# A seven-product matmul form on two of four column tiles in every pair of weight columns

## The chip, the cores and the metric

The kernel runs on one core of one Trainium2 chip. The metric is device time in microseconds for one execution, the median of several runs. The kernel before takes 2792.92 us (three runs, 2792.88 to 2793.01).

## What is computed

Two layers of a decoder trunk on 256 tokens, width 2048, all in fp32. The large products, which are nearly all of the work, are these (x is 256 x 2048):

```python
for i in range(DEPTH):                       # 2 layers
    h = rmsnorm(x, norm_mix_g[i])
    proj = h @ w_in[i]                       # conv input, q, k, v, forget logits, two gates
    y_conv = conformer_conv(...)             # ends in  u @ w_conv_out
    y_attn = forgetting_attention(...) @ w_attn_out[i]
    merged = sigmoid(g_conv) * y_conv + sigmoid(g_attn) * y_attn
    x = x + merged @ w_out[i]                # 2048 x 2048
    hf = rmsnorm(x, norm_ffn_g[i])
    gate, up = split(hf @ w_gate_up[i])      # 2 x 2048 x 5632
    x = x + (silu(gate) * up) @ w_down[i]    # 5632 x 2048
    hp = rmsnorm(x, norm_ple_g[i])
    x = x + sigmoid(hp @ w_ple_gate[i]) * (p[i] @ w_ple_proj[i])
return rmsnorm(x, final_g)
```

## The kernel before

**Tiles.** The 256 tokens are two row blocks of 128. A weight matrix is cut into column tiles of 512 columns, and each column tile into groups of 512 rows (four slices of 128 rows). A group is one load of two pieces of 128 x 1024 (two slices side by side, 512 KB), fetched on SP's queue into one of 8 `raw` tiles (line 135).

**fp32 by halves.** Every weight piece is split into a high half (ScalarE copy to `wh`, line 141, 5 buffers) and a low half (VectorE subtraction to `wl`, line 142, 5 buffers). The activations are split once in the same way. A product of a piece is then three matmuls per slice and row block: high x high (line 184), high x low (185), low x high (186), each 128 x 128 against 512 columns. I call the making of `wh` and `wl` for one piece a split.

**Plain steps.** A plain step takes one piece: two slices, two row blocks, three matmuls, so 12 matmuls for one split. A group is two plain steps per column tile.

**The seven-product form.** `fast_chunks` (line 238) does a pair of column tiles `w1`, `w2` (1024 columns) at once, into two PSUM accumulators `c1` and `c2` (one for each column tile, two banks each). Over the reduction there are groups; the text calls a group *fast* where it uses seven products of two slices for the two column tiles and two row blocks, in place of eight (the 2 x 2 form with 7 multiplications). For a fast group (lines 274 to 292) the pieces are a11, a12 (from w1), sm and a22 (from w2); GpSimd's queue adds a11 onto sm in memory by an accumulating DMA (line 276); VectorE makes two sums and one difference of pieces (lines 287, 289, 291); and seven products follow, each of one split and 6 matmuls. So a fast group is 7 splits, 3 further VectorE operations and 42 matmuls, against 4 splits and 48 matmuls for the same group in plain steps. Four products have PSUM banks of their own, `p1`, `q5`, `q6`, `q7`, which is all four banks of the pool `pms`; they are read out once per pair (lines 293 to 297) into two SBUF tiles `u1`, `u2`, and joined with `c1` and `c2` (lines 300 and 304).

**Order in a pair.** The plain steps wait in the list `left`, all of w1's first, then w2's. Inside each fast group one or two of them are put between the products (lines 280 to 283). After the last fast group, `u1` and `u2` are made, the rest of w1's steps run, `c1` is added, `first(u1)` is called, then w2's steps.

**Turns.** A result must be transposed on TensorE to be an operand of the next product: a *turn* (8 transposes of line 334 through two `pms` banks, then for a plain group a ScalarE high half and a VectorE low half, lines 321 and 322; for a group that is to be fast, `Fast.take` and `Fast.make`, lines 349 to 377, with the sums of operands). Turns wait in a queue and are run after a plain step, though not while a pair is in its fast groups (`state["quiet"]`), or at once where a step needs the operand (`await_x`, line 210).

**Who uses it.** In each layer, 24 calls of `fast_chunks`:

- mixer gates (line 850): 4 pairs, 2 fast and 2 plain groups;
- `w_out` (lines 891 to 898): 2 pairs. The operands of groups 0 and 3 of `merged` are made for the fast form; the first pair uses 1 fast group, the second 2;
- gate/up (line 925): column tiles c = 1 to 10 of the hidden width (c = 0 is done in plain steps), in three parts of 3, 4 and 4. The first tile of parts two and three (c = 3, c = 7) uses 1 fast group, the others 2;
- `w_down` (line 936): after each part, 2 pairs over that part's 3 or 4 groups. Part one uses 1 fast group in both, parts two and three use 1 in the first pair and 2 in the second;
- `w_ple_gate` (line 1000): 2 pairs, 1 fast group in the first and 2 in the second. Before each pair come two short products of 12 matmuls (`w_ple_proj`).

The Tile framework orders each engine's instructions by priority (program order) among those that its own model finds ready, so the order on an engine is near program order but not the same.

I write GU3 for the gate/up pair of c = 3, D1.0 and D1.2 for the two down pairs of part 1 (parts are 0, 1, 2), O0 and O2 for the `w_out` pairs and P0 and P2 for the PLE gate pairs.

Of the kernel before, what the change touches and what calls it, by code (L numbers as in the profile page):

```python
# [45 lines left out]
def trunk(ctx, tc, xT, xR, pT, wI, wF, wC, wA, wOut, wGU, wD, wPG, wPP, vec, bF, gF, out):  # L46
# [191 lines left out]
    def fast_chunks(fast, w1, w2, xs, ks, first, by_block=None):  # L238
# [10 lines left out]
        for w, sums in ((w1, (c11, c12)), (w2, (c21, c22))):  # L249
            for g, k0 in enumerate(ks):  # L250
                for half in range(2):
                    left.append((w[len(fast) + g][:, half * 1024 : (half + 1) * 1024], sums, k0 + 2 * half))
# [20 lines left out]
        u1, u2 = pair(), pair()  # L273
        for g, f in enumerate(fast):
# [17 lines left out]
            product(c12, f(B22), a12)  # L292
        act.activation(u1[:, 0, :], p1.t, AF.Copy)
# [5 lines left out]
        go(len(left) - 2 * len(ks))  # L299
# [245 lines left out]
    for i in range(L):  # L545
# [319 lines left out]
        fast_merged = {0: Fast(), 3: Fast()}  # L865
# [25 lines left out]
        for n in range(0, N4, 2):  # L891
            by = (0, 1, 2, 3) if n == 0 else (0, 3, 1, 2)
            onto_x(norm, n + 1)(
                fast_chunks(
                    [fast_merged[g] for g in by[: 1 + n // 2]], *([wOut[i, m][g] for g in by] for m in (n, n + 1)),
                    merged, [4 * g for g in by[1 + n // 2 :]], onto_x(norm, n),
                )
            )
# [4 lines left out]
        for part, nch in enumerate(FFN_PARTS):  # L903
            hid = {}
            fast_hid = [Fast() for _ in range(nch - 2)]
            for c in range(c0, c0 + nch):
# [10 lines left out]
                if c == 0:  # L917
                    gate(chunk(by_four(w1), norm.xs))
                    up = chunk(by_four(w2), norm.xs)
                else:  # L920
                    nf = 1 if c == c0 else 2
                    up = fast_chunks(norm.fast[:nf], w1, w2, norm.xs, range(4 * nf, KD, 4), gate)
# [8 lines left out]
            for n in range(0, N4, 2):  # L931
                await_x(hid, (4 * c0,))
                on = after if part == len(FFN_PARTS) - 1 else None
                nf = 1 if n == 0 else len(fast_hid)
                onto_x(on, n + 1)(
                    fast_chunks(
                        fast_hid[:nf], wD[i, n][c0 : c0 + nch], wD[i, n + 1][c0 : c0 + nch], hid,
                        range(4 * (c0 + nf), 4 * (c0 + nch), 4), onto_x(on, n),
                    )
                )  # L940
# [53 lines left out]
        for n in range(0, N4, 2):  # L994
            for m in range(2):
# [5 lines left out]
                norm.fast[: 1 + n // 2], wPG[i, n], wPG[i, n + 1], norm.xs, range(4 + 2 * n, KD, 4), embedded(n),  # L1001
# [65 lines left out]
```

## Time and profile before

| | |
|---|---|
| median of three runs | 2792.92 us |
| the profiled execution's own time | 2793.7 us |
| its span (first to last instruction) | 2791.8 us |
| TensorE busy | 2773.9 us, 12568 matmuls |
| VectorE busy | 2507.1 us, 3003 instructions |
| ScalarE busy | 1660.0 us, 2002 instructions |
| splits on VectorE (line 142) | 1254, 1219 ns each |
| accumulating DMAs on GpSimd's queue | 80 |
| DMA in all | 585.24 MB, 210 GB/s |

The busy time of an engine is the union of its instructions' spans. A matmul's recorded duration (about 390 ns) overlaps the next one's, so the pace of TensorE is read from starts, not from durations. A row of the stretches view gives, for one stretch of the execution, its length and then each engine's busy time in it with the count of instructions that touch it.

### The profile page before, as it was taken

Reading aid. Unit: us, or ns where it says so; the run is one execution under the profiler, and the core shown is the slowest. Engines: PE = TensorE matmul, PEld = TensorE weight load, DVE = VectorE, ACT = ScalarE, POOL = GpSimd, SP = SyncE. Lnnn points to the kernel's source line nnn. Section 1 sums busy time; section 2 is a strip of 40 time slices with the busy share of each in tenths; the row PEclk is TensorE's granted clock in tenths of the full one; section 3 lists DMA queues with packets and bytes.
Section 4 is the critical chain, followed back from the end, with each engine's and each line's share of the span. In section 5 each row is a group of like instructions: output and inputs, shape, how many; then the busy total and the mean of one; then the engine's idle time right before and its main releaser. Section 6 shows DMA issues by size and latency. Waiting matters only on the chain.

```text
span 2791.8 us, 34941 instructions
## 1 busy us (share of the span) xinstructions
PE 2773.9 (99%) x12568; PEld 2293.5 (82%) x12568; DVE 2507.1 (90%) x3003; ACT 1660.0 (59%) x2002; POOL 79.4 (3%) x121
## 2 busy tenths in 40 slices
PE   9999999999999999999999999999999999999998
PEld 7888888888888888888888888888888888888886
DVE  7999889888989988999979988988799899889998
ACT  7445766565556655656754466655665565556565
POOL 0000000000000000000000000000000000000000
PEclk9999999999999999999999999999999999999999
DMA  7555557666676766776655555575666677677674
GB/s 299 188 182 185 199 186 227 198 217 201 217 226 220 227 218 220 224 221 203 215 186 190 185 181 199 189 233 184 228 205 215 216 232 231 203 229 218 217 239 131
DMA packets 161597, 585.24 MB, mean 210 GB/s; under 512 B 18192, under 2 KB 18448, under 8 KB 161168
## 3 DMA queue, kind: packets, MB, share of 16 engines
q1 hardware_dynamic: 149040, 539.50, 56.5%
q0 software_dynamic: 11520, 41.95, 8.3%
q8 instruction: 98, 1.61, 0.2%
q10 hardware_dynamic: 864, 1.57, 0.2%
q14 instruction: 75, 0.61, 0.1%
HBM read 580.85 MB, written 2.10 MB: 209 GB/s over the span
## 4 chain that ended last, share of the span: by engine, by line
PE 93%; DVE 3%; issue 3%; ACT 1%; POOL 0%; POOLq 0%; ACTq 0%; DVEq 0%
PE mm L186 25%; PE mm L185 25%; PE mm L184 25%; PE ms L184 5%; PE ms L185 5%; PE ms L186 5%; PE ms L334 2%; DVE wl L142 1%; DVE raw L271 0%; PE ms L726 0%; ACT wh L141 0%; PE ms L755 0%; DVE pair L374 0%; PE ms L745 0%; DVE pair L271 0%
## 5 line engine op out<-in xcount | busy, mean ns | idle before, releaser
L141 ACT ACTIVATE wh<-raw 128x1024 fp32r<-128x1024 f32 x1254 | 1300.5, 1058 | 1022.7 <-PE mm L186 576.7
L142 DVE TENSOR_TENSOR wl<-raw,wh 128x1024 fp32r<-128x1024 f32 x1254 | 1501.0, 1219 | 212.4 <-ACT wh L141 204.9
L184 PE MATMUL mm<-wh,pair 128*128 128x512 f32 x3224 | 1261.9, 392 | 1.1 <-ACT pair L324 0.7
L185 PE MATMUL mm<-wl,pair 128*128 128x512 f32 x3224 | 1256.6, 390 | 0.9 <-DVE wl L142 0.8
L186 PE MATMUL mm<-wh,pair 128*128 128x512 f32 x3224 | 1256.8, 390 | 0.5 <-DVE pair L325 0.5
L186 PEld LDWEIGHTS mm<-wh,pair 128*128 128x128 f32 x3224 | 605.2, 188 | 128.4 <-DVE pair L325 1.4
L185 PEld LDWEIGHTS mm<-wl,pair 128*128 128x128 f32 x3224 | 605.6, 188 | 126.3 <-DVE wl L142 3.2
L184 PEld LDWEIGHTS mm<-wh,pair 128*128 128x128 f32 x3224 | 605.4, 188 | 126.0 <-ACT pair L324 1.7
L184 PE MATMUL ms<-wh,pair 128*128 128x512 f32 x680 | 265.7, 391 | 0.1
L186 PE MATMUL ms<-wh,pair 128*128 128x512 f32 x680 | 264.7, 389 | 0.0
L185 PE MATMUL ms<-wl,pair 128*128 128x512 f32 x680 | 264.6, 389 | 0.0
L569 DVE SCALAR_TENSOR_TENSOR pair<-pair,vecs,pair 128x256 f32<-128x256 f32 x480 | 201.1, 474 | 0.0
L271 DVE TENSOR_TENSOR raw<-raw,raw 128x1024 f32<-128x1024 f32 x160 | 195.4, 1222 | 2.6
L184 PEld LDWEIGHTS ms<-wh,pair 128*128 128x128 f32 x680 | 127.7, 188 | 28.0 <-ACT pair L998 0.9
L186 PEld LDWEIGHTS ms<-wh,pair 128*128 128x128 f32 x680 | 127.6, 188 | 26.7
L185 PEld LDWEIGHTS ms<-wl,pair 128*128 128x128 f32 x680 | 127.7, 188 | 26.0
L272 DVE TENSOR_TENSOR raw<-raw,raw 128x1024 f32<-128x1024 f32 x80 | 98.0, 1225 | 2.6
L271 DVE TENSOR_TENSOR pair<-pair,ms 128x512 f32<-128x512 f32 x144 | 93.9, 680 | 0.0
L272 DVE TENSOR_TENSOR pair<-mm,pair 128x1024 f32<-128x1024 f32 (+1 forms) x48 | 58.1, 1210 | 11.5 <-PE mm L186 11.4
L271 DVE TENSOR_TENSOR pair<-pair,mm 128x1024 f32<-128x1024 f32 x48 | 58.3, 1215 | 5.5 <-PE mm L186 5.5
L374 DVE TENSOR_TENSOR pair<-pair,pair 128x1024 fp32r<-128x1024 f32 x52 | 62.8, 1217 | 0.0
L373 ACT ACTIVATE pair<-pair 128x1024 fp32r<-128x1024 f32 x52 | 54.3, 1055 | 2.7 <-DVE pair L364 1.6
(168 smaller groups left out, 1065.0 us busy)
## 6 DMA issues: line engine op xcount, KB each, us to landing
raw<-in_wGU_dram SPq DMA_DIRECT2D x352, 512.0 KB, 4.8
raw<-in_wI_dram SPq DMA_DIRECT2D x287, 512.0 KB, 4.0
raw<-in_wD_dram SPq DMA_DIRECT2D x176, 512.0 KB, 4.8
raw<-in_wOut_dram SPq DMA_DIRECT2D x64, 512.0 KB, 4.6
raw<-in_wPG_dram SPq DMA_DIRECT2D x64, 512.0 KB, 4.9
raw<-in_wGU_dram POOLq DMA_DIRECT2D x36, 512.0 KB, 7.9
raw<-in_wA_dram SPq DMA_DIRECT2D x32, 512.0 KB, 4.7
raw<-in_wC_dram SPq DMA_DIRECT2D x32, 512.0 KB, 4.9
```

The lines of the kernel that those rows point to most:

```text
L141: act.activation(h, raw, AF.Copy)
L142: dve.tensor_tensor(l, raw, h.bitcast(F32), op=ALU.subtract)
L184: pe.matmul(self.t, lhsT=xh, rhs=wh, start=start, stop=False)
L185: pe.matmul(self.t, lhsT=xh, rhs=wl, start=False, stop=False)
L186: pe.matmul(self.t, lhsT=xl, rhs=wh, start=False, stop=self.left == 0)
L271: add = lambda o, a, b: dve.tensor_tensor(o, a, b, op=ALU.add)
L272: sub = lambda o, a, b: dve.tensor_tensor(o, a, b, op=ALU.subtract)
L334: pe.transpose(pt[:, kk * S + b * P : kk * S + (b + 1) * P], src(b)[:, c : c + P], ident)
L373: act.activation(h, t, AF.Copy)
L374: dve.tensor_tensor(l, t, h.bitcast(F32), op=ALU.subtract)
L569: dve.scalar_tensor_tensor(cv[c], u[c][:, j : j + S], w, cv[c], op0=ALU.mult, op1=ALU.add,)
```

## The change

Every pair that had one fast and three plain groups now has two and two. That is six pairs per layer: O0, GU3, GU7, D1.0, D2.0 and P0. The operands of `merged` that are made for the fast form are groups 0 and 1 rather than 0 and 3, and the `w_out` pairs take their groups in natural order. In O0, D1.0 and D2.0 (`fresh=True`) the plain steps are ordered with both column tiles' steps of the last group at the end. `u1` and `u2` are allocated after the fast groups rather than before them.

```diff
-    def fast_chunks(fast, w1, w2, xs, ks, first, by_block=None):
+    def fast_chunks(fast, w1, w2, xs, ks, first, by_block=None, fresh=False):
...
-        for w, sums in ((w1, (c11, c12)), (w2, (c21, c22))):
-            for g, k0 in enumerate(ks):
-                for half in range(2):
-                    left.append((w[len(fast) + g][:, half * 1024 : (half + 1) * 1024], sums, k0 + 2 * half))
+        order = [(w, g) for w in range(2) for g in range(len(ks))]
+        if fresh:
+            order.sort(key=lambda wg: wg[1] == len(ks) - 1)
+        for w, g in order:
+            for half in range(2):
+                src = (w1, w2)[w][len(fast) + g][:, half * 1024 : (half + 1) * 1024]
+                left.append((src, ((c11, c12), (c21, c22))[w], ks[g] + 2 * half))
...
-        u1, u2 = pair(), pair()
         for g, f in enumerate(fast):
...
+        u1, u2 = pair(), pair()
         act.activation(u1[:, 0, :], p1.t, AF.Copy)
...
-        go(len(left) - 2 * len(ks))
+        go(len(left) - 2 * (1 if fresh else len(ks)))
...
-        fast_merged = {0: Fast(), 3: Fast()}
+        fast_merged = {0: Fast(), 1: Fast()}
...
-            by = (0, 1, 2, 3) if n == 0 else (0, 3, 1, 2)
             onto_x(norm, n + 1)(
                 fast_chunks(
-                    [fast_merged[g] for g in by[: 1 + n // 2]], *([wOut[i, m][g] for g in by] for m in (n, n + 1)),
-                    merged, [4 * g for g in by[1 + n // 2 :]], onto_x(norm, n),
+                    [*fast_merged.values()], wOut[i, n], wOut[i, n + 1],
+                    merged, (8, 12), onto_x(norm, n), fresh=n == 0,
...
-                    nf = 1 if c == c0 else 2
+                    nf = 2
...
-                nf = 1 if n == 0 else len(fast_hid)
+                nf = len(fast_hid)
...
                         range(4 * (c0 + nf), 4 * (c0 + nch), 4), onto_x(on, n),
+                        fresh=n == 0 and nf == 2,
...
-                norm.fast[: 1 + n // 2], wPG[i, n], wPG[i, n + 1], norm.xs, range(4 + 2 * n, KD, 4), embedded(n),
+                norm.fast, wPG[i, n], wPG[i, n + 1], norm.xs, (8, 12), embedded(n),
```

## The prediction, made before the changed kernel was run

> **What bounds the kernel now.** I began with the page: the span, the engines and the chain of work that ended last.
>
> ```profile
> span 2791.8 us, 34941 instructions
> PE 2773.9 (99%) x12568; PEld 2293.5 (82%) x12568; DVE 2507.1 (90%) x3003; ACT 1660.0 (59%) x2002; POOL 79.4 (3%) x121
> PEclk9999999999999999999999999999999999999999
> PE 93%; DVE 3%; issue 3%; ACT 1%; POOL 0%; POOLq 0%; ACTq 0%; DVEq 0%
> ```
>
> TensorE holds 93% of the chain, at full granted clock in all slices, but VectorE is busy for 90% too. Both budgets must be read, stage by stage. The waits come next:
>
> ```profile
> ACT wh L141 <- PE mm L186: 576.7, 421, 2.7
> PEld mm L185 <- DVE wl L142: 3.2, 7, 0.9
> ```
>
> ScalarE's splits wait for TensorE to free a `wh` buffer (576.7 us in all); TensorE's loads waited for a VectorE split 7 times, 3.2 us in all. So TensorE sets the pace and the others run ahead of it to the end of their buffers. Next the stretches view, cut where pairs begin and end on TensorE. All rows but the last are of layer 0.
>
> ```profile
> core 0: us, PE busy (x) PEld busy (x) DVE busy (x) ACT busy (x) POOL busy (x), PEclk, DMA share, GB/s
> 511.87:643.00 131.13, 131.13 (x600) 108.79 (x598) 107.89 (x112) 80.72 (x102) 4.16 (x5) 1.00 0.67 210
> 790.39:832.55 42.16, 42.16 (x187) 34.92 (x186) 31.93 (x29) 21.45 (x22) 1.70 (x2) 1.00 0.72 224
> 790.39:874.28 83.89, 83.89 (x376) 69.54 (x374) 73.18 (x71) 48.86 (x51) 3.40 (x4) 1.00 0.68 214
> 874.28:916.00 41.72, 41.72 (x189) 34.61 (x188) 41.43 (x42) 27.13 (x29) 1.25 (x2) 1.00 0.72 226
> 957.77:1125.55 167.78, 167.78 (x750) 139.09 (x749) 147.59 (x141) 94.12 (x97) 5.75 (x7) 1.00 0.68 219
> 1000.86:1041.66 40.80, 40.80 (x182) 33.80 (x180) 40.11 (x37) 23.82 (x24) 0.86 (x1) 1.00 0.63 211
> 1209.07:1395.49 186.42, 185.68 (x845) 152.43 (x844) 170.99 (x177) 126.24 (x169) 5.02 (x6) 1.00 0.64 208
> 2344.82:2512.59 167.77, 167.77 (x749) 139.05 (x748) 147.59 (x141) 94.11 (x97) 5.11 (x6) 1.00 0.68 219
> ```
>
> They are: O0 to the end of c = 0's plain steps; GU3 alone; GU3 and GU4; GU5 alone; D1.0, D1.2, GU7 and GU8; D1.2 alone; D2.0 to the end of P2; and D1.0 to GU8 again in layer 1, where the length is the same to 0.01 us, so that I count both layers alike. D1.2 is a pair with two fast and two plain groups and no turn in it: 2 x 42 + 2 x 48 = 180 matmuls in 40.80 us, so **0.2267 us per matmul**. (The row's count takes in two that cross its edges.) GU5 has the same 180 plus one turn and takes 41.72. In GU5 VectorE works for 41.43 of 41.72 us and TensorE still doesn't stop: such a pair is in balance to 0.3 us. That is the closeness on which everything below turns.
>
> **The change part by part.** *Removed from TensorE.* Six pairs in each of two layers turn one plain group into a fast one: 48 matmuls become 42. 12 x 6 x 0.2267 = **16.3 us off**, all of it on the engine that sets the end. The Trainium skill ("TensorE: Matmul & The Clock Gate", Back-to-back issue gap) gives 512 / 2.4 + 2.5 = 215.8 ns for an isolated matmul; by that the saving would be 15.5 us, and the trace's 226.7 ns decides.
>
> *Added to VectorE.* Each new fast group brings 3 more splits and 3 sums or differences of pieces, all 128 x 1024.
>
> ```profile
> 884.58 9.33 DVE L142 TENSOR_TENSOR wl<-raw,wh 128x1024 fp32r<-128x1024 f32 x8
> 893.95 1.23 DVE L271 TENSOR_TENSOR raw<-raw,raw 128x1024 f32<-128x1024 f32 x1
> 895.21 1.23 DVE L272 TENSOR_TENSOR raw<-raw,raw 128x1024 f32<-128x1024 f32 x1
> 896.38 1.23 DVE L142 TENSOR_TENSOR wl<-raw,wh 128x1024 fp32r<-128x1024 f32 x1
> ```
>
> Eight splits start in 9.37 us (884.58 to 893.95), 1.17 each; the two sums take 1.26 and 1.17. Six at 1.17 = 7.0 us per changed pair, 84 us in all. With 1.4 us less TensorE time to cover it, a changed pair needs 8.4 us of VectorE's idle time. ScalarE's 3 more splits (about 1.06 us each by the row at 975.66 below) lie in its idle 41%. Idle time there is, from the rows above: O0 on, 131.13 - 107.89 = 23.2, needed 8.4; GU3 on, 10.7, needed 8.4; D1.0 on (two changed pairs), 20.2, needed 16.8; D2.0 on (D2.0 and P0), 15.4, needed 16.8. Three stretches have cover; the last is **1.4 us short**, and TensorE would wait that long, somewhere in P0 or P2. There is already one such wait in P0, which shows how thin it is:
>
> ```profile
> 1318.42 0.19 PEld L185 LDWEIGHTS mm<-wl,pair 128*128 128x128 f32 x1 [0.27 <-DVE wl L142]
> ```
>
> In layer 1 the kernel ends after P2, whose results need no turn, so I take 0.5 us there. Together 1.9 us. The bounds are 0 (the shortage is made up by work done ahead, or falls under waits that exist) and 6 (several short waits in each layer's P0 and P2).
>
> *The last operand in the three `fresh` pairs.* In O0, D1.0 and D2.0 the newest group's turn is still queued when the pair begins. Before, with one fast group, it ran after the first plain step behind the fast part, and two more steps lay before its operand was used. Now all four steps of the older plain group are used up between the seven products, and the turn, held back while the fast groups run, is followed at once by the step that needs it. Nothing else in the pair is left for TensorE: the remaining four steps all need this group, and the next pair's first split waits for a `wh` buffer that is only then freed. This is a **new wait on TensorE**. D1.0 shows what the turn costs:
>
> ```profile
> 975.23 0.40 PE L186 MATMUL mm<-wh,pair 128*128 128x512 f32 x1
> 975.46 1.04 PE L334 MATMUL ms<-ident,pair 128*128 128x128 f32 x8
> 975.66 1.06 ACT L141 ACTIVATE wh<-raw 128x1024 fp32r<-128x1024 f32 x1 [1.66 <-PE mm L186]
> 976.25 0.47 PE L184 MATMUL mm<-wh,pair 128*128 128x512 f32 x1
> 976.62 1.07 ACT L321 ACTIVATE pair<-ms 128x512 fp32r<-128x512 f32 x2
> 978.04 1.28 DVE L322 TENSOR_TENSOR pair<-ms,pair 128x512 fp32r<-128x512 f32 x2
> ```
>
> The eight transposes take TensorE from 975.46 to 976.25. The same event that ends the step before them frees a `wh` buffer, so ScalarE is in a split from 975.66 to 976.72 and makes the first high half only from 976.62, done at about 977.2 (half of 1.07). With other steps behind the transposes this costs nothing. With the operand's own step behind them, TensorE waits from 976.25 to 977.2, 0.95 us. The low half then takes 0.6 us more of VectorE, while the four weight loads with the high half can run eight matmuls (1.8 us) if they are ordered first and two (0.45 us) if not; I add 0.25. That makes 1.2 us, six times: **7.2 us**. Bounds: without the split in ScalarE's way, transposes of the first half end near 976.06 and the high half at 976.6, a wait of 0.4 each, 2.4 in all; with VectorE in the middle of other work (in the row the low half starts 1.4 us after the high) and TensorE in program order, 2.5 each, 15 in all. It can't be below nothing, since the turn isn't in this place today.
>
> *At little or no cost.* In O0 and D2.0 `first` comes with two steps left instead of six, and in P0 with four: the next norm's first turn, with its squares on ScalarE, moves towards the next pair. Its transposes wait for the residual's sum, which today costs at most this:
>
> ```profile
> PE ms L334 <- DVE xt L881: 0.7, 2, 0.4
> ```
>
> Here steps that are ready stand behind it, so I take nothing; without them it is 0.4 for each. The order of groups in `w_out` and group 1 of `merged` made fast rather than group 3: the same operations, group 1's turn under the plain steps of `w_conv_out`. Late `u1`, `u2`: no instruction more; they are first written after the fast groups in any case. The accumulating DMAs, 12 more on GpSimd's queue and none moved past another: 12 x 0.5 = 6 MB on 585, and pairs with two in a row (GU5) run unbroken. If that cover went, one landing would be seen (7.9 us by the row below) per late sum.
>
> ```profile
> raw<-in_wGU_dram POOLq DMA_DIRECT2D x36, 512.0 KB, 7.9
> ```
>
> *Sum.* 16.3 - 7.2 - 1.9 = 7.2 us less. The profiled execution's own time is 2793.7 (span 2791.8 and 1.9 around it), 0.8 above the median of the runs; so a span near 2784.6, an execution near 2786.5, and a median of 2792.9 - 7.2 = **2785.7**.
>
> **The rivals.** *The wait is filled* (chance 0.20). If the scheduler finds room for the transposes among the last products (the bank of `p1` is read early), or other work behind them, the full 16.3 less some 2 comes: 2776.6 to 2781. For it: an engine's order is not strictly program order. Against: in D1.0 the turn stands exactly at its place behind the first free step, not earlier.
>
> *Longer waits* (0.15). At the upper bounds 16.3 - 15 - 4 = 2.7 slower: 2789 to 2796. For it: the 1.4 us between high and low half in the row above.
>
> *VectorE can't save its idle time* (0.10). The place is O0, D2.0 and P0. A split can be at most five `wh` and `wl` buffers ahead of its use, so idle time outside a pair helps only as far as that lead reaches. In their own stretches these three have less than 8.4:
>
> ```profile
> 511.87:555.99 44.12, 44.12 (x203) 36.47 (x202) 39.98 (x42) 27.70 (x34) 1.70 (x2) 1.00 0.69 208
> 1209.07:1253.05 43.98, 43.98 (x204) 36.55 (x203) 37.96 (x39) 25.61 (x32) 1.70 (x2) 1.00 0.71 223
> 1302.86:1346.53 43.67, 43.63 (x196) 35.51 (x195) 36.73 (x40) 28.89 (x39) 1.60 (x2) 1.00 0.69 228
> ```
>
> Idle 4.1, 6.0 and 6.9: short by 4.3, 2.4 and 1.5, 8.2 a layer, 16.4 in all, which eats the whole saving; with the 7.2 of the turns the kernel is 7.3 slower: **2800.2**. It decides where the lead with which VectorE enters such a pair is smaller than the shortage. Against it: GU5 has next to no idle time of its own and TensorE doesn't wait. The Trainium skill ("VectorE: DVE Perf Modes", The DRAIN you can't avoid) says that the next VectorE operation doesn't start until the pipe is empty; then each of the 72 added operations would hold the engine for its full 1.22 us, 88 us, and GU5 would be out of balance today. The eight splits above, started 1.17 apart, do not agree with it.
>
> *It changes nothing* (0.05): the time saved in GU3, GU7 and P0 is lost at the next place where VectorE is late; within 3 us of 2792.9.
>
> **How the numbers follow.** The forecast (0.50) has its own range 2782 to 2789. A measurement of this kernel tells about 0.2% from no change, 5.6 us, that is 2787.3. Of the forecast 0.8 lies below it (0.40), and the filled wait wholly (0.20): faster 0.60. Same: 0.10 of the forecast, 0.12 of the longer waits and 0.05: 0.27. Slower: 0.03 and 0.10: 0.13. The range 2777 to 2796 leaves out the slower rival and the last of the full saving.
>
> **What would show it.** Right: 72 matmuls less (12496), VectorE's busy time up by some 80 us; GU3 and GU7 at 40.8 us (from 42.16) without a wait; in O0, D1.0 and D2.0 a wait of about 1.2 us before line 184 or 186, ended by ScalarE or VectorE on line 321 or 322; small waits for line 142 in P0 or P2 of layer 0. Wrong: no such wait (then about 2777), waits for line 142 in O0 or D2.0 (VectorE is the bound), or the accumulating DMAs ending waits of splits.

## The result: slower, and the profile after

The changed kernel takes 2807.95 us (median of four runs, 2806.72 to 2811.41) against 2792.90 (four runs, 2792.59 to 2793.01): 15.0 us more, a ratio of 1.0056 with a 95% interval of 1.0039 to 1.0073. The forecast was 2785.7 with a range of 2777 to 2796, so both the size and the direction were wrong. The profiled execution took 2808.98.

First the page: the span, the engines, the granted clock, and the chain of work that ended last.

```profile
span 2807.3 us, 34968 instructions
PE 2768.3 (99%) x12496; PEld 2282.9 (81%) x12496; DVE 2586.8 (92%) x3075; ACT 1693.5 (60%) x2038; POOL 89.6 (3%) x133
PEclk9999999999999999999999999999999999999999
PE 84%; DVE 9%; issue 5%; ACT 2%; POOL 0%; ACTq 0%; POOLq 0%; DVEq 0%
```

The change did what it says: 72 matmuls fewer (12568 to 12496), and VectorE's busy time is up by 79.7 us, as forecast. But TensorE holds 84% of the chain in place of 93%; VectorE has 9% and "issue" 5%. The 16.3 us came off, and 31.3 us of other time was put on. TensorE's waits in the waits view (engine, line, what it waited for: us in total, times, longest) show where to look:

```profile
PE mm L186 <- DVE pair L326: 5.8, 6, 1.0
PE mm L184 <- ACT wh L141: 4.4, 5, 1.6
PE ms L338 <- DVE xt L885: 3.4, 2, 1.7
PE mm L184 <- ACT pair L325: 3.0, 4, 0.8
PE ms L184 <- ACT wh L141: 2.2, 6, 0.4
PE ms L338 <- DVE xt L970: 1.8, 1, 1.8
```

(Lines up to the fast groups keep their numbers or move by 1 to 4; the halves of a turn, 321 and 322 before, are 325 and 326, the transposes 338, the residual's sums 885 and 970.) Two of the six are the forecast's wait, an operand's high half (325) and low half (326): 8.8 us. The others are not in the forecast: splits that ScalarE makes late (141), and transposes that wait for a residual's sum (885, 970). Before, the largest wait for a residual's sum was 0.4. The slices of the page hide one thing more: three stretches of 3.41 us, from 1305.08, 1359.69 and 2639.69 us, have a granted clock of 0.50, where the kernel before has none ahead of its last 9 us.

To see which pair pays, I cut both traces at the same matmuls, by counting them. The table has the length before and the difference to it in the changed kernel and in four of the kernels below; a changed pair that lost nothing would show -1.36. PP0 to PP3 are the short products ahead of P0 and P2. Where a step or a turn's transposes have moved across such a boundary, two neighbouring rows share one difference and only their sum means something: D1.0 with D1.2, PP1 with P0, and in layer 0 PP2+PP3 with P2. What is not listed differs by 0.13 or less, but for GU6 (+0.3 in some columns) and the last product ahead of the mixer's second gate in layer 1 (-0.2 in all).

| layer.pair | before | after | early turn | + old order | + P0 back | + turn one product later |
|---|---|---|---|---|---|---|
| 0.O0 / 1.O0 | 44.13 / 44.17 | +0.66 / +0.60 | -1.09 / -0.92 | -1.01 / -1.05 | -1.00 / -1.04 | -1.01 / -1.07 |
| 0.O2 / 1.O2 | 42.59 / 42.61 | +1.85 / +2.10 | +1.82 / +1.77 | +1.56 / +0.73 | +1.51 / +0.73 | +0.73 / +0.73 |
| GU3, GU7 (four) | 42.16 | -1.36 | -1.36 | -1.36 | -1.36 | -1.36 |
| 0.D1.0 / 1.D1.0 | 43.09 | +0.29 / +0.30 | -0.93 / -0.91 | -0.91 / -0.91 | -0.91 / -0.92 | -0.91 / -0.91 |
| D1.2 (two) | 40.80 | +0.45 | 0 | 0 | 0 | 0 |
| 0.D2.0 / 1.D2.0 | 43.98 / 43.99 | +1.02 / +2.54 | -0.09 / -0.19 | -0.81 / -0.82 | -0.84 / -0.85 | -0.82 / -0.82 |
| 0.D2.2 / 1.D2.2 | 42.59 | +1.85 / +1.86 | +1.78 / +1.79 | +1.31 / +0.97 | +0.96 / +2.06 | +0.97 / +1.25 |
| 0.PP1 / 1.PP1 | 4.50 / 4.51 | +2.80 / +1.54 | +2.80 / +3.07 | +1.24 / +1.22 | +1.24 / +1.24 | -2.14 / -2.15 |
| 0.P0 / 1.P0 | 43.67 / 42.70 | -2.07 / -1.89 | -2.08 / -1.86 | -2.05 / -1.90 | -0.52 / -0.52 | +1.12 / +1.11 |
| 0.PP2+PP3 | 5.44 | +6.37 | +6.46 | +6.71 | 0 | 0 |
| 0.P2 / 1.P2 and end | 43.53 / 53.70 | -1.71 / +1.76 | -1.77 / +1.73 | -0.93 / +1.77 | +0.02 / -0.03 | +0.01 / -0.01 |

The column after adds up to 15.3 us; the spans differ by 15.5. Only GU3 and GU7 keep their whole gain, and the stretches view shows it for GU3 (length, then busy time of TensorE, weight loads, VectorE and ScalarE, with counts):

```profile
792.98:833.78 40.80, 40.80 (x182) 33.78 (x180) 38.47 (x35) 24.74 (x25) 1.27 (x2) 1.00 0.75 230
```

40.80 us without a gap, as forecast, with VectorE at 38.47 of them. Two of the losses are in pairs that had two fast groups already: O2 and D2.2 are each about 1.9 us longer with the same matmuls. What was put on them was moved there.

**The operand's turn in O0.** The timeline (start, us, engine, line, what, and in brackets the idle time and what ended it):

```profile
541.90 1.03 PE L338 MATMUL ms<-ident,pair 128*128 128x128 f32 x8
542.10 1.06 ACT L141 ACTIVATE wh<-raw 128x1024 fp32r<-128x1024 f32 x1 [0.30 <-PE mm L186]
543.07 1.07 ACT L325 ACTIVATE pair<-ms 128x512 fp32r<-128x512 f32 x2
543.70 0.50 PE L184 MATMUL mm<-wh,pair 128*128 128x512 f32 x1 [0.76 <-ACT pair L325]
543.81 1.28 DVE L275 TENSOR_TENSOR pair<-pair,ms 128x512 f32<-128x512 f32 x2
545.00 1.28 DVE L326 TENSOR_TENSOR pair<-ms,pair 128x512 fp32r<-128x512 f32 x2
545.75 0.50 PE L186 MATMUL mm<-wh,pair 128*128 128x512 f32 x1 [0.83 <-DVE pair L326]
```

The first half is as forecast: a split (141) stands in front of the high halves and TensorE waits 0.76 us. Then comes what I had left to a 0.25 addition: VectorE's list has two of the four sums that make `u1` and `u2` (275, from 543.81) ahead of the low halves (326, from 545.00), and TensorE, which by then has only four matmuls that need no low half, waits another 0.83 us. So 1.6 us by the gaps, not 1.2.

**The turn that slid into O2.** With `first` called two steps before the pair's end, the next norm's first turn is issued where O2's fast groups begin:

```profile
560.31 2.35 DVE L378 TENSOR_TENSOR pair<-pair,pair 128x1024 fp32r<-128x1024 f32 x2
562.58 2.35 DVE L142 TENSOR_TENSOR wl<-raw,wh 128x1024 fp32r<-128x1024 f32 x2
564.97 1.22 DVE L275 TENSOR_TENSOR raw<-raw,raw 128x1024 f32<-128x1024 f32 x1
566.28 1.07 ACT L141 ACTIVATE wh<-raw 128x1024 fp32r<-128x1024 f32 x1 [3.89 <-DVE raw L275]
568.66 0.50 PE L184 MATMUL ms<-wh,pair 128*128 128x512 f32 x1 [0.42 <-ACT wh L141]
570.95 0.50 PE L184 MATMUL mm<-wh,pair 128*128 128x512 f32 x1 [0.62 <-ACT wh L141]
```

O2 begins at 556.77. In the kernel before it began at 555.99, and there the same turn's low halves (374) were done before it, so that the first sum of pieces (271) stood 4.9 us behind its start and not 8.2:

```profile
550.34 2.35 DVE L374 TENSOR_TENSOR pair<-pair,pair 128x1024 fp32r<-128x1024 f32 x2
560.85 1.22 DVE L271 TENSOR_TENSOR raw<-raw,raw 128x1024 f32<-128x1024 f32 x1
```

In the changed kernel VectorE makes the low halves of that turn (378), then two splits, and only then the sum of pieces (275) that a product waits for. ScalarE stood idle for 3.89 us until that sum, its split came late, and so did two products. TensorE's transposes had cost next to nothing, which is what I had looked at; the price is on VectorE's list.

### The profile page after: what moved, and what is told of

Read it like the earlier page. It is cut to its first block, busy times and chain, and to the rows that moved or that the text cites. A ratio compares the mean times of both kernels' runs of the same rounds, so it can differ in the third digit from the quotient of the medians.

```text
span 2807.3 us, 34968 instructions
## 1 busy us (share of the span) xinstructions
PE 2768.3 (99%) x12496; PEld 2282.9 (81%) x12496; DVE 2586.8 (92%) x3075; ACT 1693.5 (60%) x2038; POOL 89.6 (3%) x133
## 4 chain that ended last, share of the span: by engine, by line
PE 84%; DVE 9%; issue 5%; ACT 2%; POOL 0%; ACTq 0%; POOLq 0%; DVEq 0%
PE mm L186 22%; PE mm L185 22%; PE mm L184 22%; PE ms L185 5%; PE ms L186 5%; PE ms L184 5%; DVE wl L142 4%; DVE raw L275 2%; PE ms L338 2%; ACT wh L141 1%; DVE raw L276 1%; DVE pair L275 1%; DVE pair L378 1%; PE ms L730 0%; DVE xt L885 0%
## 5 line engine op out<-in xcount | busy, mean ns | idle before, releaser
L141 ACT ACTIVATE wh<-raw 128x1024 fp32r<-128x1024 f32 x1290 | 1334.5, 1058 | 998.8 <-PE mm L186 487.3
L142 DVE TENSOR_TENSOR wl<-raw,wh 128x1024 fp32r<-128x1024 f32 x1290 | 1539.9, 1220 | 155.7 <-ACT wh L141 147.8
L184 PE MATMUL mm<-wh,pair 128*128 128x512 f32 x3104 | 1216.7, 392 | 8.5 <-ACT wh L141 4.4
L186 PE MATMUL mm<-wh,pair 128*128 128x512 f32 x3104 | 1211.2, 391 | 6.3 <-DVE pair L326 5.8
L185 PE MATMUL mm<-wl,pair 128*128 128x512 f32 x3104 | 1212.5, 391 | 0.9 <-DVE wl L142 0.8
L184 PEld LDWEIGHTS mm<-wh,pair 128*128 128x128 f32 x3104 | 583.5, 188 | 133.2 <-ACT wh L141 7.6
L186 PEld LDWEIGHTS mm<-wh,pair 128*128 128x128 f32 x3104 | 583.8, 188 | 131.3 <-DVE pair L326 8.7
L184 PE MATMUL ms<-wh,pair 128*128 128x512 f32 x776 | 303.6, 391 | 2.2 <-ACT wh L141 2.2
L185 PE MATMUL ms<-wl,pair 128*128 128x512 f32 x776 | 302.1, 389 | 0.0
L186 PE MATMUL ms<-wh,pair 128*128 128x512 f32 x776 | 302.0, 389 | 0.0
L275 DVE TENSOR_TENSOR raw<-raw,raw 128x1024 f32<-128x1024 f32 x184 | 224.8, 1222 | 3.0
L184 PEld LDWEIGHTS ms<-wh,pair 128*128 128x128 f32 x776 | 145.8, 188 | 34.8 <-ACT wh L141 4.9
L186 PEld LDWEIGHTS ms<-wh,pair 128*128 128x128 f32 x776 | 145.7, 188 | 30.4
L276 DVE TENSOR_TENSOR raw<-raw,raw 128x1024 f32<-128x1024 f32 x92 | 112.7, 1225 | 3.0
L279 POOL DMA_DIRECT2D raw<-in_wGU_dram x40 | 34.2, 855 | 792.4 <-DVE wl L142 448.5
```

Source lines behind the costliest of these rows:

```text
L141: act.activation(h, raw, AF.Copy)
L142: dve.tensor_tensor(l, raw, h.bitcast(F32), op=ALU.subtract)
L184: pe.matmul(self.t, lhsT=xh, rhs=wh, start=start, stop=False)
L185: pe.matmul(self.t, lhsT=xh, rhs=wl, start=False, stop=False)
L186: pe.matmul(self.t, lhsT=xl, rhs=wh, start=False, stop=self.left == 0)
L275: add = lambda o, a, b: dve.tensor_tensor(o, a, b, op=ALU.add)
```

## The experiments

Theory W says that the loss is a set of waits at places which the new order makes: the turn that is used at once, the turn that slid into O2 and D2.2, and the short products ahead of P0 and P2. Theory V is the rival on VectorE: it is late by the 7.0 us that it has to do more in each changed pair, whatever the order. Later two narrower theories came in: C on the clock and P on a place in TensorE's list. A half-rate window, in the expectations, is a stretch of 3.41 us whose granted clock is 0.50 in the trace. Unless a text names another, each kernel was timed in five rounds beside the kernel before, which gave 2792.62 to 2792.68.

**One part alone.** GU3 and GU7 changed in the kernel before, and nothing else:

```diff
-                    nf = 1 if c == c0 else 2
+                    nf = 2
```

> The kernel before with one edit: GU3 and GU7 use two fast groups, nothing else is changed. Theory W (the loss is made of waits at three places: the last operand's turn in the fresh pairs, the next norm's first turn that slid into the fast groups of O2 and D2.2, and VectorE late around P0): this part has none of them, so 24 matmuls less at 0.2267 us, 5.4 us faster than before, near 2787.5, GU3 and GU7 at 40.8 us each. Theory V (VectorE is simply the bound, wherever a fast group is added): at least 2792.9, with waits of TensorE for line 142 in or behind GU3 and GU7.

Measured: 2787.17 (2787.04 to 2787.84), ratio 0.998 (0.9971 to 0.9989): 5.5 us less for 24 matmuls fewer, 5.44 by count. The four times 7.0 us that VectorE has to do more are wholly hidden here. Next O0, D1.0 and D2.0 alone, by taking GU3, GU7 and P0 back:

```diff
-                    nf = 2
+                    nf = 1 if c == c0 else 2
...
-                norm.fast, wPG[i, n], wPG[i, n + 1], norm.xs, (8, 12), embedded(n),
+                norm.fast[: 1 + n // 2], wPG[i, n], wPG[i, n + 1], norm.xs, range(4 + 2 * n, KD, 4), embedded(n),
```

> The changed kernel with GU3, GU7 and P0 put back to one fast group: only O0, D1.0 and D2.0 are changed. Theory W: 36 matmuls less save 8.2 us; against it six waits for the last operand at about 1.8 us (10.9), the four slid turns at 1.4 (5.4), and some of the late VectorE before P0 with a half-rate clock window (3 to 5): 11 to 13 slower than before, 2804 to 2806. Theory V: three of six changed pairs, about half of the 15 us: near 2800.

Measured: 2809.58, ratio 1.0059 (1.0046 to 1.0071): 17.0 slower, more than either theory gave. And P0 alone, the second of those two edits in the other direction on the kernel before:

> The kernel before with one edit: P0 uses two fast groups. Theory W: VectorE comes to P0 no later than in the kernel before, so the 2.7 us of matmuls are won less a wait of 1 to 2 us in P2 of the first layer: 2790.5 to 2792.5. Theory V: P0 lies in the stretch with the least idle time of VectorE (8.9 us for 8.4 needed) and should be slower than before by 1 to 4 us: 2794 to 2797.

Measured: 2794.68, ratio 1.0007 (0.9998 to 1.0016): 2.1 us more where 2.7 less were to be had. W's range was missed and V's held, though W's wait is there, alone and large:

```profile
1353.69 1.06 PE L334 MATMUL ms<-ident,xt 128*128 128x128 f32 x8 [1.75 <-DVE xt L966]
1355.33 0.63 PE L186 MATMUL mm<-wh,pair 128*128 128x512 f32 x1
1355.75 0.63 PE L184 MATMUL mm<-wh,pair 128*128 128x512 f32 x1
```

The wait lies in the short products ahead of P2 in layer 0, and right behind it matmuls start 0.42 us apart in place of 0.2267, which led to theory C below. GU3 and GU7 gain 5.5, O0, D1.0 and D2.0 lose 17.0, P0 loses 2.1; together 13.6 of the 15.0.

**The operand's turn.** One line lets the turn of the last operand run inside the first fast group, with everything else as changed:

```diff
-            if nk == 8 and len(fast) == 1:
+            if nk == 8 and len(fast) == 1 or fresh and g == 0:
                 run()
```

> The changed kernel with the queued turn run in the first fast group of a fresh pair (before the product q7) instead of just ahead of the step that needs it; VectorE's work is the same. Theory W: the waits on lines 325 and 326 go (10.5 us in the profile) and with them one of three half-rate clock windows: 2796 to 2798. Theory V: the same VectorE work, so no change: 2806 to 2809.

Measured: 2797.46, ratio 1.0017 (1.0009 to 1.0026): 10.5 us less, as W said. The waits for lines 325 and 326 are gone from the view, and in the table O0, D1.0, D2.0 and D1.2 give 10.4 us back between them. The profiled execution, the slowest of its eleven, still has three stretches at half clock, so that part of W's expectation did not come. To see whether those waits needed a busy VectorE, the next kernel is the changed one with VectorE relieved (six low halves of the second fast group left out: `product` takes `wh` for `wl` there):

```diff
+            low = not (g == 1 and (fresh or lean))
...
-            product(q7, f(T3), sm)
+            product(q7, f(T3), sm, low)
```

> The changed kernel (2808) with the same six low halves left out in O0, D1.0, D2.0 and P0: VectorE is relieved of its added time there, and the place of the operand's turn stays. Theory W (a turn that is used at once costs its own way through transposes, ScalarE and VectorE, whatever VectorE's load): the six waits on the operand's halves stay at 1.5 to 2 us each turn, 2790 to 2795, some 10 to 14 us above the kernel with the early turn and the same left out. Rival (the operand's halves were late only because VectorE was): those waits fall below 0.5 each, 2780 to 2784.

Measured: 2805.96, ratio 1.0048 (1.0035 to 1.0061). The totals that I gave were too low for both theories (only 2.0 us went), but the waits answer the question; line 328 and 329 are the high and low halves of this kernel:

```profile
PE mm L188 <- DVE pair L329: 4.5, 6, 0.8
PE mm L186 <- ACT pair L328: 3.2, 4, 0.8
```

7.7 us where the changed kernel has 8.8. VectorE's load is little of what makes the turn late; its way through transposes, ScalarE, four sums and VectorE is.

**The half clock.** In the kernel with O0, D1.0 and D2.0 alone two stretches of 3.41 us have a granted clock of 0.50. The stretches view of the two, each with the stretch ahead of it (length, TensorE, weight loads, VectorE, ScalarE and GpSimd busy, granted clock, DMA share, GB/s):

```profile
541.99:545.41 3.42, 1.81 (x7) 1.16 (x7) 3.42 (x6) 1.27 (x3) 0.00 (x0) 1.00 0.93 232
545.44:548.85 3.41, 3.41 (x10) 2.64 (x9) 1.10 (x1) 0.00 (x0) 0.00 (x0) 0.50 1.02 347
...
2637.80:2641.20 3.40, 1.60 (x8) 0.84 (x7) 3.40 (x6) 1.48 (x3) 0.00 (x0) 1.00 0.92 222
2641.22:2644.63 3.41, 3.41 (x9) 2.67 (x10) 1.53 (x2) 0.00 (x0) 0.00 (x0) 0.50 1.02 308
```

TensorE was busy for 1.81 and 1.60 of the 3.4 us ahead. Theory C takes that for the cause. The test fills the wait with work that changes nothing: the second half's transposes are done twice more in this turn.

```diff
+            for _ in range(repeat[0] if half == 1 else 0):
+                for kk in range(2):
+                    for b in range(2):
+                        c = (2 * half + kk) * P
+                        pe.transpose(pt[:, kk * S + b * P : kk * S + (b + 1) * P], src(b)[:, c : c + P], ident)
```

> The kernel with two fast groups in O0, D1.0 and D2.0 (GU and P0 as before), with the four transposes of the second half done twice more in the fresh turn: eight further transposes, to the same result, which lie in TensorE's wait for the operand halves. Theory C (the half-rate windows follow a window in which TensorE was busy for about half of it or less): no half-rate window in the profile, the waits on L326 alike or up to 0.3 us each longer, 2806 to 2808. Theory W without C (the waits alone cost, the clock drops are chance): the drops stay, 2809 to 2811.

Measured: 2807.01 (2806.59 to 2808.52) against 2809.58 without the filling (another set of runs, beside the same 2792.6 of before): 2.6 us less with 48 transposes more. The same stretch of O0, and one of layer 1:

```profile
541.90:545.30 3.40, 2.56 (x17) 1.91 (x15) 3.40 (x6) 1.65 (x3) 0.00 (x0) 1.00 0.98 254
545.30:548.70 3.40, 3.40 (x16) 2.75 (x16) 1.42 (x2) 1.02 (x1) 0.00 (x0) 1.00 1.01 355
2698.07:2701.48 3.41, 1.66 (x10) 1.14 (x10) 3.41 (x4) 2.22 (x6) 0.00 (x0) 1.00 0.77 297
2701.48:2704.89 3.41, 3.41 (x9) 2.68 (x9) 3.25 (x7) 3.29 (x7) 0.72 (x1) 0.50 0.44 144
```

With 2.56 of 3.40 us busy the clock stays whole and 16 matmuls run where 10 did. Layer 0's O0 is 44.81 us long in place of 46.36, and layer 1's D2.0 44.93 in place of 46.57. The same pairs of the other layer, which had no half-rate stretch in either kernel, are as long as that in both (44.77, and 44.97 and 44.96). So one such stretch costs 1.6 us. The expectation of none was too bold: one came up in layer 1's short products (last two rows), which were not filled and where TensorE had been busy for 1.66 of 3.41. The waits here are as long as before the filling; it is the clock that was bought. Two of six such turns had a half-rate stretch without the filling and none of six with it, in one execution of each, so this pair of kernels alone could be chance; the count over all kernels, in the last section, is the stronger evidence.

**Order and tiles.** The early turn and, besides, the old order of plain steps (w1's, then w2's), with which `first` comes with four steps left:

```diff
-        if fresh:
-            order.sort(key=lambda wg: wg[1] == len(ks) - 1)
...
-        go(len(left) - 2 * (1 if fresh else len(ks)))
+        go(len(left) - 2 * len(ks))
```

> The changed kernel with the early turn of the run before and, besides, the plain steps of all pairs in the old order (w1's first, then w2's), so that c1 and the next norm's first turn come two steps earlier in O0 and D2.0. Theory W: the waits of 0.6 and 0.8 us for line 141 in O2 and D2.2 (four pairs, 5.4 us) go: 2791 to 2793. If instead the length of these waits comes only from VectorE's amount of work (theory V): 2796 to 2799 as with the early turn alone.

Measured: 2792.64, ratio 0.9998 (0.999 to 1.0007): 4.8 us less again, as W said, and no difference to the kernel before is left. The places are not quite W's. In the two profiled executions, which lie 6.2 apart, O2 and D2.2 get 2.6 us (W had 5.4 there), D2.0 1.4 and PP1 3.4, and P2 of layer 0 gives 0.8 back. In PP1 most of it is the clock: the kernel with the early turn has a half-rate stretch there in both layers, this one has none. Allocating `u1` and `u2` early again in the changed kernel:

> The changed kernel with u1 and u2 allocated before the fast groups again. Theory W: they are written after the fast groups in any case, so no difference: 2806.5 to 2809.5. Rival: the late allocation takes or gives time by another buffer and another order: more than 3 us to either side.

Measured: 2808.43 (2807.8 to 2808.73), ratio 1.0056 (1.0042 to 1.007): the late tiles cost and save nothing, as both sides of the forecast had it.

**P0.** The kernel with the early turn and the old order, with one fast group in P0 as before:

> As the run with the old order and the early turn, and P0 back to one fast group: what is left is GU3, GU7, O0, D1.0 and D2.0 with two, 60 matmuls less than before (13.6 us). Theory W: P0 costs 2 to 4 us net, so 2788 to 2790, and about 2780 if the waits before P0 vanish too. Theory V: VectorE has 70 us more work than before: not below 2792.

Measured: 2788.68, ratio 0.9986 (0.9978 to 0.9995). So P0's edit costs 4.0 us net here, where it cost 2.1 alone. P0 in the last layer alone, on the kernel before:

```diff
-                norm.fast[: 1 + n // 2], wPG[i, n], wPG[i, n + 1], norm.xs, range(4 + 2 * n, KD, 4), embedded(n),
+                norm.fast if last else norm.fast[: 1 + n // 2], wPG[i, n], wPG[i, n + 1], norm.xs,
+                (8, 12) if last else range(4 + 2 * n, KD, 4), embedded(n),
```

> The kernel before with P0 at two fast groups in the last layer only, where no turn of the result follows. Theory W (the loss of P0 in both layers, 2.1 us, is the turn of its result waiting in front of P2, with a half-rate clock window behind it): 6 matmuls less and nothing against it, 1.4 us faster, near 2791.3. Theory V (VectorE has too little idle time around P0): 1 us slower, near 2793.6.

Measured: 2793.16, ratio 1.0001 (0.9992 to 1.001): nothing gained, and V's 2793.6 is nearer than W's 2791.3. But it is no wait of TensorE: its last matmul starts at 2776.81 us in place of 2778.63, 1.8 earlier (0.6 of it already where O0 of layer 0 begins, ahead of any difference between the two). The timeline of ScalarE at the end, of this kernel and then of the kernel before:

```profile
2778.93 1.33 ACT L991 ACTIVATE xt<-xt,rt 128x512 f32<-128x512 f32 x2 [1.86 <-POOL rt L448]
2780.69 0.72 ACT L963 ACTIVATE pair<-pair,rt 128x512 f32<-128x512 f32 x1 [0.43 <-ACT xt L991]
```

```profile
2779.91 0.72 ACT L963 ACTIVATE pair<-pair,rt 128x512 f32<-128x512 f32 x1 [0.75 <-DVE pair L272]
2781.82 1.34 ACT L991 ACTIVATE xt<-xt,rt 128x512 f32<-128x512 f32 x2 [1.19 <-POOL rt L448]
```

The last block's sigmoid (963) now stands behind the first block's scaling (991), where it stood ahead of it; the end of the kernel is 1.1 us longer after the last matmul. Over all the kernels of this document the two go together: with one fast group in P0 of the last layer the sigmoid comes first and the end takes 13.1 us from the start of the last matmul, with two the scaling comes first and it takes 14.2 to 14.5. In layer 0 the turn between the two short products ahead of P2 can be issued later, which is the edit here (on the kernel before with P0 alone):

```diff
-            run()
+            if turn:
+                run()
...
-                for b, t in enumerate(chunk([(wPP[i, n + m], range(2))], ps)):
+                for b, t in enumerate(chunk([(wPP[i, n + m], range(2))], ps, turn=n == 0)):
```

> The kernel before with P0 in two fast groups, and the turn that lay inside the two short products ahead of P2 issued later, after P2's fast groups. Theory W (P0 pays by the 1.75 us wait of the transposes in the short phase and by the half-rate window behind it): both go in the first layer, 2791 to 2792.2; the last layer keeps its longer tail (about 1.6). Rival (VectorE is late by then whatever is issued first, the wait moves to the next reader): 2794 to 2796.

Measured: 2793.50, ratio 1.0003 (0.9995 to 1.0012), between the two expectations: 1.2 us less than with P0 alone. The wait of 1.75 and the half-rate stretch are gone, and smaller waits stand in their place:

```profile
PE mm L185 <- DVE wl L142: 1.9, 4, 0.9
PE mm L184 <- ACT wh L141: 0.6, 1, 0.6
```

Some of P0's loss was a bad place, and some is VectorE and ScalarE, which by then are late for whoever comes first. This is the stretch that the forecast had found 1.4 us short; whether the added splits are what makes it late, the kernels without their low halves tell below.

**VectorE's share.** With the early turn and the old order, O2, D2.2 and the short products still cost more than their count. The first try moved VectorE's four operand sums of the norms' turns to GpSimd (in `make`, `eng.tensor_tensor` with `eng` GpSimd for turns with gains):

> The kernel with all changed pairs, the old order of plain steps and the early turn (2792.6), with the four operand sums of each fast turn of the norms (the ones with gains) on GpSimd in place of VectorE: VectorE has 4 operations less per such turn. Theory V (what is left at O2, D2.2 and ahead of P0 is VectorE that is late by its added 7.0 us per pair): those three places lose half or more of their waits, 2787 to 2790. Rival (the waits are for one chain of raw sum, split and product, however early VectorE is; or GpSimd is slower at the sums and becomes the late one): 2792 to 2796.

Measured: 2819.59, ratio 1.0098 (1.0085 to 1.0112), and no answer to the question: GpSimd takes 1.2 to 1.4 us on average for a sum that takes VectorE 0.42 in the kernel before, ScalarE is then late behind it, and four waits of up to 4.4 us follow.

```profile
L366 POOL TENSOR_TENSOR pair<-pair 128x256 f32<-128x256 f32 x24 | 32.9, 1372 | 121.4 <-ACT pair L360 121.4
L366 POOL TENSOR_TENSOR pair<-pair,pair 128x256 f32<-128x256 f32 x24 | 28.7, 1196 | 1.1 <-ACT pair L360 0.3
...
PE ms L184 <- ACT wh L141: 17.4, 4, 4.4
```

The second try leaves the low halves out, as above, and with them VectorE's added splits:

> The kernel with all changed pairs but P0, the old order and the early turn (2788.7), with six of the seven low halves of the second fast group of O0, D1.0 and D2.0 left out (the high half is used in their place): about 7.0 us less of VectorE in each of those pairs, the matmuls, the sums of pieces and the high halves as they are. Theory V (VectorE's debt): O2, D2.2 and the short products ahead of P0 come back to their lengths of before, and O0 and D2.0 to 1.36 shorter than before; about 9 us less, 2779 to 2781. Rival (the chain of raw sum, high half and product): these places keep their 1 to 1.5 each, 2787 to 2789.

> The kernel with all changed pairs, the old order and the early turn (2792.6), with the same six low halves left out in O0, D1.0, D2.0 and P0. Theory V: all 16.3 us of matmuls are seen but for the longer tail of the last layer (1.6): 2777 to 2780. Rival: the waits at O2, D2.2 and ahead of P0 and P2 stay, with the half-rate window, 2788 to 2792.

Measured: 2786.22, ratio 0.9976 (0.9967 to 0.9985), and 2790.13, ratio 0.9991 (0.9982 to 1.0): 2.5 us less than their full kernels, both: nearer to the rival in the first, inside the rival's range in the second. V's 9 us did not come. Cut as in the table, O2 and D2.2 fall to +0.6 each in both layers, and D2.0 and O0 hardly move. So VectorE's lateness is real, 2.5 us of it. P0 costs 3.9 us net between these two kernels, where it cost 4.0 with all low halves made, and in the second the waits of P0's stretch are still there:

```profile
PE ms L339 <- DVE xt L971: 1.8, 1, 1.8
PE mm L186 <- ACT wh L140: 1.4, 1, 1.4
```

Six low halves less are about the 7.0 us of VectorE that the second fast group adds, so P0's loss is not made by that added work. What stays elsewhere is in the waits view of the first of the two:

```profile
PE ms L339 <- DVE xt L886: 2.7, 2, 1.4
```

**A place in TensorE's list.** These are the transposes of the norm's last turn, ahead of P0. In the changed kernel:

```profile
1301.94 0.39 PE L186 MATMUL ms<-wh,pair 128*128 128x512 f32 x1
1302.17 0.76 PE L184 MATMUL mm<-wh,pair 128*128 128x512 f32 x2
1303.36 1.22 DVE L885 TENSOR_TENSOR xt<-xt,pair 128x1024 f32<-128x1024 f32 x1
1304.63 0.55 PE L338 MATMUL ms<-ident,xt 128*128 128x128 f32 x3 [1.71 <-DVE xt L885]
```

Two matmuls lie between the first short product and the transposes. In the kernel before there were seven (a product and the first matmul of a plain step of P0, which the framework puts there), and the wait was 0.35:

```profile
1299.19 1.21 DVE L881 TENSOR_TENSOR xt<-xt,pair 128x1024 f32<-128x1024 f32 x1
1300.46 0.77 PE L334 MATMUL ms<-ident,xt 128*128 128x128 f32 x5 [0.35 <-DVE xt L881]
```

The source has the same order in both. Theory P says that this place is what counts; the turn is issued one short product later:

```diff
-                for b, t in enumerate(chunk([(wPP[i, n + m], range(2))], ps)):
+                for b, t in enumerate(chunk([(wPP[i, n + m], range(2))], ps, turn=n + m > 0)):
```

> The kernel with all changed pairs but P0, the old order and the early turn (2788.7), with the last turn of the norm issued behind the second of the two short products ahead of P0, not behind the first. Theory P (the place on TensorE): the two waits of 1.35 us on the residual's sum (both layers) go, nothing takes their place, 2785.5 to 2786.5. Rival (what is late is the way through sum, transposes, halves and product, so that the wait moves to P0's first user of this turn): 2788 to 2789.5.

Measured: 2784.80, ratio 0.9972 (0.9961 to 0.9983): 3.9 us less, more than P's 2.2 to 3.2. The transposes now follow thirteen other matmuls and wait for nothing:

```profile
1295.62 1.21 DVE L884 TENSOR_TENSOR xt<-xt,pair 128x1024 f32<-128x1024 f32 x1
...
1297.77 1.04 PE L337 MATMUL ms<-ident,xt 128*128 128x128 f32 x8
```

**The parts that pay.** GU3 and GU7 with D1.0 (early turn, old order), everything else as in the kernel before:

```diff
-                nf = len(fast_hid)
+                nf = 1 if n == 0 and on is not None else len(fast_hid)
```

> The kernel before, with two fast groups in GU3 and GU7 and in D1.0 alone (D1.0 with the order of plain steps of before and the turn of the next half issued inside the first fast group). O0, O2, D1.2, D2.0, D2.2, P0 and P2 stay as before. Theory W (an edit gains where VectorE has idle time behind it and no short phase follows): 2787.2 less two times 0.91, 2785.2 to 2785.7, each D1.0 0.9 us shorter than before and what follows it unchanged. Theory V (VectorE's work is only put off, and comes back one pair later): D1.0 0.9 shorter, D1.2 longer by as much, 2787.0 to 2787.5.

Measured: 2785.57 (2785.17 to 2785.97), ratio 0.9975 (0.9966 to 0.9985), W's number: each D1.0 is 0.9 shorter and D1.2 pays nothing for it. And the same with the turn one short product later:

> The kernel with two fast groups in GU3, GU7 and D1.0 alone (2785.6), with the same turn behind the second short product. The wait of 0.35 us that the kernel before has there goes in both layers: 2784.6 to 2785.4; if the turn comes too late for P0, 2785.6 to 2787.

Measured: 2783.21 (2782.84 to 2783.81), ratio 0.9966 (0.9954 to 0.9978): 9.4 us less than the kernel before, the best of all. The gain of 2.4 over the kernel without the later turn was expected at 0.2 to 1.0; PP1 and P0 together are 1.2 shorter in each layer. The 0.35 that I had taken from the kernel before was the gap alone; the matmuls around the transposes start late there as well.

## Why the prediction was wrong, point by point

*Removed from TensorE, 16.3 us:* right. 72 matmuls went, and GU3 and GU7 show -1.36 each without a gap, four times.

*The operand's turn, 7.2 us:* the mechanism was right and its size was off. Moving the turn away gave 10.5 us back, 1.75 for each, inside the bounds of 0.4 to 2.5. The term that was too small is the low half: I put it at 0.25 beyond the high half, and it is 0.8 to 1.0 (5.8 us over the six turns against 1.5), while the high half's wait came out smaller than priced (3.0 against 5.7). The low half is late since VectorE's list has two 0.6 us sums ahead of it. Part of the 10.5 is the half clock that such a wait can bring, 1.6 us each time.

*At little or no cost, nothing:* this is the step that failed, a term put at nothing for a reason that held on one engine. "Its transposes wait for the residual's sum ... Here steps that are ready stand behind it, so I take nothing" looked at TensorE alone. The moved turn brings four sums and two low halves of 1.2 us for VectorE (about 4 us in the list of O2's start), and these now stood in front of the sums and splits of the next pair's fast groups. The old order gave 4.8 us back, on top of the early turn, a part of it half-rate stretches that no longer came in PP1. (That edit puts back the order of the plain steps and the place of the turn together; the rows of VectorE point to the turn, and no run parts the two.) This step alone does not turn the sign. From the forecast's 7.2 less to the measured 15.0 more are about 22 us: 3.3 are the operand's turn beyond its 7.2, 4.8 this step, 4.8 P0 beyond its 1.9, and some 9.7 that no term of the forecast held and that the sum below takes apart.

*VectorE's shortage, 1.9 us in P0 and P2:* the place was right, the price too low, and the mechanism mostly another. P0 costs 4.0 net, so 6.7 against its 2.7 saved, and 3.9 net without the low halves of its added splits, so it isn't their time on VectorE that was short. The largest parts seen are a wait of 1.75 for the residual's sum and, with the other edits, one of 1.4 to 1.7 for a split of ScalarE, in a phase of 12-matmul products that offers little else to do; the half clock behind them; and a tail that is 1.1 to 1.4 us longer, with ScalarE's order at the end turned round. The waits that the forecast named grew by little: TensorE's weight loads waited for a split's low half (142) for 4.1 us in all in the changed kernel, 3.2 before. I had given half a microsecond to the last layer because "the kernel ends after P2, whose results need no turn"; that end alone takes back 1.1 of its gain of 1.4.

*VectorE can't save its idle time (the rival on the slower side):* the result lies 7.8 us above its 2800.2, and its mechanism was mostly not the cause. VectorE's added splits are worth 2.5 us where the rival had 16.4.

*Longer waits, 2789 to 2796:* nearest in kind, but its upper bounds held one turn per pair and no moved one. *The wait is filled:* it was not, by the 8.8 us of waits for the operand's halves.

*Late tiles, accumulating DMAs, the order of groups in `w_out`:* right at nothing for the tiles. For the DMAs no wait in the views above is theirs. The order of groups was not run alone.

The 31.3 us that came on, then: 10.5 the turn that is used at once, 4.8 the order that moved the norm's turn, 6.7 P0, and 9.7 that the kernel with one fast group in P0 still lacks to its count (60 x 0.2267 = 13.6, less 3.95 seen); the four add up to 31.7, which is as near as medians of different sets of runs come. Of the 9.7, 2.5 are VectorE's splits by the kernel without them. The turn ahead of P0 gave 3.9, of which the kernel with D1.0 could have had 2.4 too, so 1.5 belong to the change. O0, D1.0 and D2.0 stay 0.3 to 0.5 us above -1.36 with the early turn and the old order, 2.6 in all, and O2 and D2.2 0.6 each above the length before even without the added splits, 2.3. These last two I did not take apart, and why the framework put two matmuls and not seven ahead of P0's transposes was not settled either.

## What to carry to other kernels

A turn or a reduction that is moved is priced on every engine that it passes through, by what then stands behind it on that engine's list, and not by its own time on the engine that sets the pace; here a move that put 4 us of VectorE ahead of the next pair's first splits went with a loss of 4.8 us, while the 28 us that GU3 and GU7 added cost nothing. A saving is taken pair by pair: two of the six edits paid in full and a third, D1.0, by two thirds, and keeping only those made a kernel that is faster by 7.1 us, or 9.4 with the one turn put later, where the whole was slower by 15.0. And the phases to look at first are the short ones, with only a dozen matmuls between two dependences, and the end.

## What the runs showed of the hardware

A wait can cost TensorE twice. The granted clock changes in steps of 3.41 us. Inside the runs the clock fell from full to half 21 times, over ten kernels, each time behind a stretch of that length in which TensorE was busy for 0.04 to 0.53 of the time (0.53, 0.47 and 0.49 in the rows above). Behind stretches at full clock that were busy for 0.56 or more it never fell, and five between 0.50 and 0.55 kept it, so the edge is near one half. Four times a second stretch at half clock followed, in two of them although TensorE had been busy for 0.68 and 0.75 of the first. At half clock matmuls start 0.42 to 0.43 us apart, and the two measured stretches cost 1.6 us each. The Trainium skill ("TensorE: Matmul & The Clock Gate", Part 1: The HAM clock gate) has the clock go down after at least one idle window of about 3.4 us, and gives 426.7 ns between cold matmuls of 512 columns. The spacing agrees with the runs here. The condition does not: in the rows above TensorE was idle for only half of such a window.
